# Groups of seven split b right behind a and use it second; landed tiles' splits stand in line in w_down's first units

## The chip, the cores and the metric

The kernel runs on one core of one Trainium2 chip. The metric is device microseconds of one execution of the whole program. The engines that count here are TensorE (PE), VectorE (DVE), ScalarE (ACT), GpSimd (POOL) and SyncE (SP, which issues most transfers). Each engine works through its own list of instructions in program order; semaphores make one engine wait for another. Weights come from DRAM by DMA. SBUF is the on-chip memory of 128 partitions, PSUM the memory in which matmuls accumulate, used in banks of 128 x 512 f32.

## The reference

One decoder layer for one sequence of 256 tokens, model width 2048, all f32:

```python
def reference(x, ...):
    mix = hybrid_mixer(rmsnorm(h, norm_mix_pre), w_in, ..., w_out)   # state-space heads beside attention heads
    h = h + rmsnorm(mix, norm_mix_post)
    ff = squared_relu_mlp(rmsnorm(h, norm_mlp_pre), w_up, w_down)
    h = h + rmsnorm(ff, norm_mlp_post)

def squared_relu_mlp(u, w_up, w_down):
    hdn = jax.nn.relu(jnp.einsum('bsd,df->bsf', u, w_up))            # 2048 -> 8192
    return jnp.einsum('bsf,fd->bsd', hdn * hdn, w_down)              # 8192 -> 2048
```

Most of the work is matmuls with large f32 weights that are each used for 256 tokens only (w_in, w_out, w_up, w_down).

## The kernel before

**Products in three parts.** A weight tile `raw` (two blocks of 128 rows by 512 columns, `[128, 2, 512]`) is split into `hi`, a rounded copy made by ACT (L150), and `lo = raw - hi`, made by DVE (L151). Activations lie as pairs too: `ah/al`, `sh/sl` or `ua`. A product is three matmuls of 128x512: hi with a_h, lo with a_h, hi with a_l. `parts` gives hi and lo from rings of 5 buffers each. Weights land in a ring of 4 `raw` buffers and in whatever other SBUF tiles are free at that time (`room["raw"]`: `mw`, `ha`, `uc` and so on), taken by turn in `fetch_next`; a buffer's next transfer waits until its last reader is done.

**Units.** The function `unit` computes two neighbouring blocks of 512 output columns for both tiles of 128 tokens. It goes over steps of 256 input rows in a written order. A step is either direct (`row_tiles`, L382 to L384: two weight tiles and 24 matmuls) or a group of seven (`seven`): the 2x2x2 blocks of weight and activation are combined so that seven products of 21 matmuls (L469 to L471) do the work of eight. The up units have 7 planned steps of which four are groups of seven, and one last direct step; the first units of w_down have 14 planned steps with six groups of seven and two last direct steps.

**A group of seven** needs these operands of the two weight tiles raw_a and raw_b. The first half of raw_b does not come from the weight as it is: POOL adds two blocks of rows in a DRAM tile called `pair`, and raw_b fetches that sum, so it can be used as it lands.

- a: raw_a, two halves; b: raw_b, two halves (the DRAM sum and a plain block)
- e: two differences that DVE makes (L275): e[1] = raw_a[0] + raw_b[0], then e[0] = e[1] - raw_b[1]
- t: t4 = e[1] + raw_a[1] (L275, `r<-e,raw` in the trace)

Each is split by `split_in_line`. `in_line` chains these instructions: each is issued on ACT and DVE behind the one chained before it, whatever the scheduler would prefer. Four products start sums of their own in `more[0..3]` and run through all groups of seven of a unit; the other three add into `acc`, where the direct steps add too. Behind the last group of seven, `combine_new` (L478 to L482) or `combine_onto` (L1152 to L1160) distributes `more[0..3]`: first a copy of more[0], then a subtraction of more[2], then more[3] and more[1].

**Activations of a group of seven** are combined as well (`sums_of_acts`, L428 to L431 on DVE, and a split), one step ahead.

**Hidden activations.** At the end of an up unit `up_end` puts a generator `turned` into `beside` for each block of 128 tokens by 512 columns: relu (L1522), square (L1523) and a 16-bit copy (L1515) on ACT, a transposing DMA from SP, and after its `yield`, a copy back (L1515) and the split into `ah/al` (L150 and L151), from which w_down's matmuls read. `pump_beside` runs the first half of one, `land_beside` the second, at the steps in TURNS and LANDS. In the first units of w_down the copies are placed exactly (`room["exact"]`): they are chained by `in_line`, between a group's splits and the next step's. The split behind the copy back is not: the scheduler places it among all that is ready. In half 1 the `halves` buffers of `turned` are parts of an SBUF tile `ha`, which later joins the ring of weight buffers (`more_in_place`), and a weight's transfer into it waits for the last al split that reads it.

The program runs the up units and two w_down units for one half of the 8192 hidden columns, then again for the other half. The six groups of seven of w_down's first unit start on PE between 953.8 (the first) and 1005.8 us (the last) in half 0, and between 1288.8 and 1347.9 in half 1.

Of the kernel before, what the change touches and what calls it, by code (L numbers as in the profile page):

```python
# [10 lines left out]
F32 = mybir.dt.float32  # L11
# [33 lines left out]
AHEAD = 1_000_000  # L45
# [35 lines left out]
def hymba_layer(ctx: ExitStack, tc: tile.TileContext, x, norm_mix_pre, w_in, conv_w, conv_b, dt_bias, a_log,  # L81
# [34 lines left out]
    def part(k):  # L116
        if k < NK:
            return sh, sl, k
        i, r = divmod(k - NK, NK // 2)
        return (*att[i], r)  # L120
# [14 lines left out]
    def bank():  # L135
        return pacc.tile([P, NB], F32, name="acc")

    def psmall():
        return psm.tile([P, NB], F32, name="ps")
# [7 lines left out]
    def split(hi, lo, src, scale=None):  # L147

        if scale is None:
            return (nc.scalar.activation(hi, src, AF.Copy),  # L150
                    nc.vector.tensor_tensor(lo, src, hi.bitcast(F32), op=ALU.subtract))  # L151
        return (nc.scalar.activation(hi, src, AF.Copy, scale=scale),
                nc.vector.scalar_tensor_tensor(lo, src, scale, hi.bitcast(F32), op0=ALU.mult, op1=ALU.subtract))
# [16 lines left out]
    def tmp():  # L170
        if "own" in room:
            room["own"].rotate(1)
            return room["own"][0]
        return hp.tile([P, NB], F32, name="r", bufs=4)

    def sum_tile():
        return room["sum"] if "own" in room else hp.tile([P, KB, NB], F32, name="e")
# [3 lines left out]
    room = {}  # L181
# [52 lines left out]
    def fetch_next(src, k0, c0, pair=None):  # L234

        turn = room["turn"]
        room["turn"] += 1
        n = turn % (RAWS + len(room["raw"])) - RAWS
        into = None if turn < 0 or n < 0 else room["raw"][n]
        with ExitStack() as order:  # L240
            for last in loaded if room.get("chain") else ():
                order.enter_context(tc.issue_after(last.ins))
            return fetch(src, k0, c0, into=into, pair=pair)

    def parts():
        return [wp.tile([P, KB, NB], F32R, name=n, bufs=BUFS) for n in ("hi", "lo")]
# [13 lines left out]
    @contextmanager  # L260
    def in_line():

        with ExitStack() as order:
            for last in line.values():
                order.enter_context(tc.issue_after(last.ins))
            yield

    def split_in_line(hi, lo, raw):
        with in_line():
            line["act"], line["dve"] = split(hi, lo, raw)  # L270
            newest["act"] = line["act"]

    def add_in_line(dst, a, b, op=ALU.add):
        with in_line():
            line["dve"] = nc.vector.tensor_tensor(dst, a, b, op=op)  # L275
# [33 lines left out]
    def pair_of(src, ca, k):  # L309

        next_pair()
        s_, c_, k_, d = paired[turn_of["pair"]]
        assert (s_ is src) and (c_, k_) == (ca, k), (c_, k_, ca, k)
        turn_of["pair"] += 1
        return d
# [103 lines left out]
    def sums_of_acts(k):  # L419

        if k in sums_of:
            return sums_of[k]
        places = room["sums"][2 * len(sums_of):][:2]
        h_, l_, r = room["acts"](k * KB)
        with tc.high_priority(offset=AHEAD):
            a, c = (tmp().rearrange("p (i s) -> p i s", s=P) for _ in range(2))
            ah_, al_ = (v[:, r:r + KB].bitcast(F32).rearrange("p j (t s) -> p j t s", t=NT) for v in (h_, l_))
            nc.vector.tensor_tensor(a.rearrange("p (j t) s -> p j t s", t=NT), ah_, al_, op=ALU.add)  # L428
            nc.vector.tensor_tensor(c[:, 0:2], a[:, 0::3], a[:, 1:2].to_broadcast([P, 2, P]), op=ALU.subtract)
            nc.vector.tensor_tensor(c[:, 2], a[:, 0], c[:, 1], op=ALU.add)  # L430
            nc.vector.tensor_tensor(c[:, 3], a[:, 2], c[:, 2], op=ALU.subtract)  # L431
            ch, cl = (v.rearrange("p b (t s) -> p (b t) s", t=NT) for v in places)
            split(ch, cl, c)
        sums_of[k] = ch, cl
        return ch, cl

    def seven(src, ca, cb, k, acc, more, first, last):


        ch, cl = sums_of_acts(k)  # L440
        h_, l_, r = room["acts"](k * KB)
        with tc.high_priority(offset=AHEAD):
            raw_a = fetch_next(src, k * KB, ca)
            raw_b = fetch_next(src, k * KB, cb, pair_of(src, ca, k))
            e, t4 = sum_tile(), tmp()
            add_in_line(e[:, 1], raw_a[:, 0], raw_b[:, 0])
            add_in_line(e[:, 0], e[:, 1], raw_b[:, 1], ALU.subtract)
            hl_a = parts()
            split_in_line(*hl_a, raw_a)
            add_in_line(t4, e[:, 1], raw_a[:, 1])  # L450
            hl_e = parts()
            split_in_line(*hl_e, e)
            hl_b = parts()
            split_in_line(*hl_b, raw_b)
            hl_t = parts()
            split_in_line(*(v[:, 0] for v in hl_t), t4)

        def block(j, t):
            return tuple(v[:, r + j, t * P:(t + 1) * P] for v in (h_, l_))

        def summed(i):
            return ch[:, i], cl[:, i]

        for dst, (a_h, a_l), (hi, lo), j, own in (
                (more[0], block(0, 0), hl_a, 0, True), (acc[0], block(1, 0), hl_a, 1, False),
                (more[1], summed(1), hl_e, 0, True), (more[2], summed(2), hl_e, 1, True),
                (more[3], summed(0), hl_b, 0, True), (acc[1], summed(3), hl_b, 1, False),
                (acc[2], block(1, 1), hl_t, 0, False)):
            nc.tensor.matmul(dst, a_h, hi[:, j], start=own and first, stop=False)  # L469
            nc.tensor.matmul(dst, a_h, lo[:, j], start=False, stop=False)  # L470
            nc.tensor.matmul(dst, a_l, hi[:, j], start=False, stop=own and last)  # L471
# [74 lines left out]
    def gemm_features(src, c0, begun=None, pumps=(1,)):  # L546


        acc = features()
        for k0 in range(0, NK, KB):  # L550
            hi, lo = weights(src, k0, c0) if k0 or begun is None else begun

            edges = k0 in (0, NK - KB)
            for fs in [(f,) for f in range(4)] if edges else [range(4)]:
                products(acc, hi, lo, k0, [(f, j) for f in fs for j in range(KB)])
            pump(pumps[k0 // KB % len(pumps)])
        return acc
# [397 lines left out]
    def attention(ap, h, qT, kT, v):  # L955
# [30 lines left out]
        for j, p in enumerate(turned):  # L986
            pair[j] = ap.tile([P, 3 * P], F32, name="pT", bufs=4)
            nc.scalar.activation(pair[j], p[:, :3 * P], AF.Copy)
# [343 lines left out]
    acc = [bank() for _ in range(2 * NT)]  # L1332
# [44 lines left out]
    more = [psmall(), bank(), psmall(), bank()]  # L1377
# [12 lines left out]
    acc, more = more, acc  # L1390
# [109 lines left out]
    def up_end(fb, b):  # L1500

        def at_end(t, acc):
            with tc.high_priority(offset=AHEAD):
                r = room["shared"][b][t]
                nc.vector.tensor_tensor(r, acc, r, op=ALU.subtract if b else ALU.add)
            beside.append(turned(t, 4 * fb, r))
        return at_end

    def perhaps_in_line(dst, src):

        if not room["exact"]:
            nc.scalar.activation(dst, src, AF.Copy)
            return
        with tc.high_priority(offset=AHEAD), in_line():
            newest["act"] = line["act"] = nc.scalar.activation(dst, src, AF.Copy)  # L1515

    def turned(t, k, r):
        room["halves"].rotate(1)
        halves = room["halves"][0]
        ts = slice(t * P, (t + 1) * P)  # L1520
        words = r.bitcast(U16)
        nc.scalar.activation(r, r, AF.Relu, scale=rmlp[:, t:t + 1])  # L1522
        nc.scalar.activation(r, r, AF.Square)  # L1523
        perhaps_in_line(halves.rearrange("p (h n) -> p h n", h=2), words.rearrange("p (n h) -> p h n", h=2))
        nc.sync.dma_start_transpose(words.rearrange("p (n s) -> p n s", s=P), halves)
        yield
        perhaps_in_line(halves.rearrange("p (n h) -> p h n", h=2), words.rearrange("p (h n) -> p h n", h=2))
        d_h, d_l, i = part(k)
        split(d_h[:, i:i + 4, ts], d_l[:, i:i + 4, ts], halves.bitcast(F32).rearrange("p (f s) -> p f s", f=4))

    def onto_new_mw(more):

# [6 lines left out]
    acc = gemm_features(w_up, NB, begun)  # L1539
# [6 lines left out]
    acc, more = [bank() for _ in range(2 * NT)], [psmall(), bank(), psmall(), bank()]  # L1546
    for hf in range(2):
        if hf:
            beside_up([], 0)
        for fb in range(0 if hf else 2, 8, 2):  # L1550
# [4 lines left out]
            acc, more = more, acc  # L1555
# [75 lines left out]
```

## Time and profile before

| | |
|---|---|
| median of 3 runs | 1460.96 us (1460.77 to 1460.99) |
| the profiled execution's own time | 1460.29 us |
| its span on the core | 1458.5 us |
| mean granted TensorE clock | 0.996 |
| DMA | 340.30 MB, mean 233 GB/s |
| groups of seven | 87, of 21 matmuls each |

The profile is one execution, taken by the hardware profiler. The page lists busy time of each engine, the span in 40 slices, the chain of work that ended last and the costliest groups of instructions. A row of the timeline reads: start in us, length in us, engine, line, operation, output<-inputs, shape, count; in brackets the idle time of the engine ahead of it and what ended it. Matmul ends are modelled, so a matmul's length is read from the distance between two starts. A window row reads: from and to in us, length, busy us and instructions of PE, its weight loads, DVE, ACT and POOL, the granted clock, the share of the DMA engines and GB/s.

### The profile page before, as it was taken

To read this page: it belongs to the slowest core of one execution; us is meant where nothing else is said; L and a number is where in the kernel's file an instruction comes from. 1 tells how busy PE (TensorE), PEld (TensorE's weight loads), DVE (VectorE), ACT (ScalarE), POOL (GpSimd) and SP (SyncE) were. 2 spreads that over 40 slices of the span, in tenths; PEclk is the share of its full clock that TensorE was granted. 3 is DMA by queue.
4 is the path that set the end of the run, shared out by engine and by line. 5 is a ranking of instruction groups with operands and counts; after the bars stand their busy time and mean duration, and the time that the engine had idled before them with its cause. 6 is when DMAs were issued, how large, how long until landed. Compare 5 with 4: busy or idle time off the path is not lost.

```text
span 1458.5 us, 20230 instructions
## 1 busy us (share of the span) xinstructions
PE 1437.7 (99%) x6930; PEld 1207.1 (83%) x6930; DVE 1297.9 (89%) x1881; ACT 1001.3 (69%) x1407; POOL 162.3 (11%) x244
## 2 busy tenths in 40 slices
PE   9999999999999999999999999999999999998998
PEld 8888888888888888888888888887888888876786
DVE  6798888988999788689989999999889999987998
ACT  6577669666666666566657679976565799876564
POOL 0201110131111000011100111010111111001000
PEclk9999999999999999999999999999999999999999
DMA  7977656756888647588976799698788999998855
GB/s 256 276 218 225 186 173 185 238 173 195 235 249 244 196 131 237 183 270 262 267 232 211 222 342 291 186 256 273 203 252 263 266 268 278 254 259 250 275 181 173
DMA packets 201926, 340.30 MB, mean 233 GB/s; under 512 B 45616, under 2 KB 48544, under 8 KB 201824
## 3 DMA queue, kind: packets, MB, share of 16 engines
q1 hardware_dynamic: 174304, 279.72, 61.4%
q0 software_dynamic: 19648, 45.63, 15.5%
q10 hardware_dynamic: 7872, 13.68, 2.8%
q8 instruction: 54, 0.88, 0.2%
q14 instruction: 48, 0.39, 0.1%
HBM read 327.39 MB, written 49.84 MB: 259 GB/s over the span
## 4 chain that ended last, share of the span: by engine, by line
PE 65%; DVE 6%; ACT 3%; issue 2%; DMA 2%; SPq 0%; DVEq 0%; ACTq 0%
PE acc L384 9%; PE acc L382 9%; PE acc L383 9%; PE acc L469 6%; PE acc L470 6%; PE acc L471 6%; PE acc L540 4%; DVE lo L151 3%; PE ps L384 2%; PE ps L382 2%; PE ps L383 2%; PE acc L543 2%; PE ps L471 2%; PE ps L470 2%; PE ps L469 2%
## 5 line engine op out<-in xcount | busy, mean ns | idle before, releaser
L151 DVE TENSOR_TENSOR lo<-raw,hi 128x1024 fp32r<-128x1024 f32 (+1 forms) x392 | 475.4, 1217 | 84.6 <-ACT hi L150 82.5
L150 ACT ACTIVATE hi<-raw 128x1024 fp32r<-128x1024 f32 (+1 forms) x392 | 408.0, 1048 | 181.6 <-PE acc L384 58.1
L540 PE MATMUL acc<-ua,hi 128*128 128x512 f32 x520 | 142.1, 402 | 0.0
L150 ACT ACTIVATE hi<-e 128x1024 fp32r<-128x1024 f32 x66 | 70.0, 1061 | 61.0 <-DVE e L275 55.5
L540 PEld LDWEIGHTS acc<-ua,hi 128*128 128x128 f32 x520 | 91.8, 190 | 14.1
L382 PE MATMUL acc<-hi,ua 128*128 128x512 f32 x228 | 90.0, 395 | 0.0
L383 PE MATMUL acc<-lo,ua 128*128 128x512 f32 x228 | 89.2, 391 | 0.0
L384 PE MATMUL acc<-hi,ua 128*128 128x512 f32 x228 | 89.1, 391 | 0.0
L382 PE MATMUL acc<-hi,sh 128*128 128x512 f32 x220 | 86.4, 393 | 0.0
L384 PE MATMUL acc<-hi,sl 128*128 128x512 f32 x220 | 85.7, 389 | 0.0
L383 PE MATMUL acc<-lo,sh 128*128 128x512 f32 x220 | 85.6, 389 | 0.0
L543 PEld LDWEIGHTS acc<-ua,lo 128*128 128x128 f32 x520 | 77.0, 190 | 9.0
L151 DVE TENSOR_TENSOR lo<-e,hi 128x1024 fp32r<-128x1024 f32 x66 | 80.4, 1217 | 0.9 <-ACT hi L150 0.7
L543 PE MATMUL acc<-ua,lo 128*128 128x256 f32 x520 | 79.2, 282 | 0.0
L469 PE MATMUL acc<-hi,ah 128*128 128x512 f32 x180 | 70.1, 390 | 4.1 <-ACT hi L150 4.1
L470 PE MATMUL acc<-lo,ah 128*128 128x512 f32 x180 | 70.4, 391 | 0.0
L471 PE MATMUL acc<-hi,al 128*128 128x512 f32 x180 | 70.3, 390 | 0.0
L540 PE MATMUL acc<-uc,hi 128*128 128x512 f32 x208 | 61.4, 405 | 0.0
L150 ACT ACTIVATE hi<-ha 128x1024 fp32r<-128x1024 f32 x46 | 48.2, 1051 | 15.8 <-DMA ha<-in_w_down_dram 6.2
L151 DVE TENSOR_TENSOR lo<-ha,hi 128x1024 fp32r<-128x1024 f32 x46 | 55.7, 1218 | 2.7 <-ACT hi L150 2.6
L150 ACT ACTIVATE hi<-r 128x512 fp32r<-128x512 f32 x66 | 41.2, 625 | 18.3 <-PE acc L384 8.5
L469 PE MATMUL acc<-hi,ua 128*128 128x512 f32 x137 | 53.5, 390 | 0.0
(578 smaller groups left out, 3739.0 us busy)
## 6 DMA issues: line engine op xcount, KB each, us to landing
raw<-in_w_in_dram SPq DMA_DIRECT2D x154, 512.0 KB, 4.6
raw<-in_w_down_dram SPq DMA_DIRECT2D x70, 512.0 KB, 5.4
raw<-in_w_up_dram SPq DMA_DIRECT2D x65, 512.0 KB, 5.1
raw<-in_w_out_dram SPq DMA_DIRECT2D x38, 512.0 KB, 5.1
raw<-pair SPq DMA_DIRECT2D x61, 256.0 KB, 4.3
pair<-in_w_up_dram POOLq DMA_DIRECT2D x56, 256.0 KB, 6.1
pair<-in_w_down_dram POOLq DMA_DIRECT2D x52, 256.0 KB, 5.8
ha<-in_w_up_dram SPq DMA_DIRECT2D x25, 512.0 KB, 5.7
```

What stands on the lines that cost most here:

```text
L150: return (nc.scalar.activation(hi, src, AF.Copy), nc.vector.tensor_tensor(lo, src, hi.bitcast(F32), op=ALU.subtract))
L151: nc.vector.tensor_tensor(lo, src, hi.bitcast(F32), op=ALU.subtract))
L382: nc.tensor.matmul(dst[:, cs], a_h[:, r, ts], hi[:, j, cs], start=begin and j == 0, stop=False)
L383: nc.tensor.matmul(dst[:, cs], a_h[:, r, ts], lo[:, j, cs], start=False, stop=False)
L384: product[t] = nc.tensor.matmul(dst[:, cs], a_l[:, r, ts], hi[:, j, cs], start=False, stop=end and j == KB - 1)
L469: nc.tensor.matmul(dst, a_h, hi[:, j], start=own and first, stop=False)
L470: nc.tensor.matmul(dst, a_h, lo[:, j], start=False, stop=False)
L471: nc.tensor.matmul(dst, a_l, hi[:, j], start=False, stop=own and last)
L540: nc.tensor.matmul(acc[f], hi[:, j, f * P:(f + 1) * P], u(k0 + j), start=k0 + j == 0, stop=False, skip_group_check=True)
L543: nc.tensor.matmul(acc[f][:, 0], lo[:, j, f * P:(f + 1) * P], u(k0 + j)[:, 0], start=False, stop=k0 + j == NK - 1, skip_group_check=True)
```

## The change

In `seven` the split of raw_b moves from behind the split of e to directly behind the split of raw_a, ahead of t4's addition. On PE the two products with b become the third and fourth, the two with e the fifth and sixth. In `turned`, where placement is exact, the split behind the copy back becomes a `split_in_line` at high priority: ah directly behind the copy on ACT, al directly behind the DVE instruction chained last. No operand, product or transfer is added or removed.

```diff
@@ seven
             hl_a = parts()
             split_in_line(*hl_a, raw_a)
+            hl_b = parts()
+            split_in_line(*hl_b, raw_b)
             add_in_line(t4, e[:, 1], raw_a[:, 1])
             hl_e = parts()
             split_in_line(*hl_e, e)
-            hl_b = parts()
-            split_in_line(*hl_b, raw_b)
             hl_t = parts()
             split_in_line(*(v[:, 0] for v in hl_t), t4)
...
                 (more[0], block(0, 0), hl_a, 0, True), (acc[0], block(1, 0), hl_a, 1, False),
+                (more[3], summed(0), hl_b, 0, True), (acc[1], summed(3), hl_b, 1, False),
                 (more[1], summed(1), hl_e, 0, True), (more[2], summed(2), hl_e, 1, True),
-                (more[3], summed(0), hl_b, 0, True), (acc[1], summed(3), hl_b, 1, False),
                 (acc[2], block(1, 1), hl_t, 0, False)):
@@ turned
-        split(d_h[:, i:i + 4, ts], d_l[:, i:i + 4, ts], halves.bitcast(F32).rearrange("p (f s) -> p f s", f=4))
+        whole = halves.bitcast(F32).rearrange("p (f s) -> p f s", f=4)
+        if not room["exact"]:
+            split(d_h[:, i:i + 4, ts], d_l[:, i:i + 4, ts], whole)
+            return
+        with tc.high_priority(offset=AHEAD):
+            split_in_line(d_h[:, i:i + 4, ts], d_l[:, i:i + 4, ts], whole)
```

How this moves instructions is seen in the order in which each engine gets them. First ACT in the first w_down unit of half 0, from the splits of one group of seven to the next step's split; `hi<-e` and `hi<-r` are the splits of e and t4, the `hi<-raw` next to `hi<-e` that of raw_b, and the two L1515 rows the copy back of one landing tile and the copy of the next tile to be turned. Before:

```order
L150 ACTIVATE hi<-raw 128x1024
L150 ACTIVATE hi<-e 128x1024
L150 ACTIVATE hi<-raw 128x1024
L150 ACTIVATE hi<-r 128x512
L1515 ACTIVATE mw_6209<-hb 128x2x512
L1522 ACTIVATE wpost<-wpost,rmlp 128x512
L150 ACTIVATE ah_3798<-mw_6209 128x4x128
L1523 ACTIVATE wpost<-wpost 128x512
L1515 ACTIVATE mw_6209<-wpost 128x1024
L150 ACTIVATE hi<-raw 128x1024
```

And now:

```order
L150 ACTIVATE hi<-raw 128x1024 x2
L150 ACTIVATE hi<-e 128x1024
L150 ACTIVATE hi<-r 128x512
L1515 ACTIVATE mw_6209<-hb 128x2x512
L150 ACTIVATE ah_3798<-mw_6209 128x4x128
L1522 ACTIVATE wpost<-wpost,rmlp 128x512
L1523 ACTIVATE wpost<-wpost 128x512
L1515 ACTIVATE mw_6209<-wpost 128x1024
L150 ACTIVATE hi<-raw 128x1024
```

The split of raw_b moved ahead of that of e, and ah moved ahead of the relu of the next tile.

Second, DVE in the last group of seven of that unit and behind it; `al` is the low part of landed tiles, L479 the first subtraction of `combine_new`. Before:

```order
L275 TENSOR_TENSOR r<-e,raw 128x512
L151 TENSOR_TENSOR lo<-e,hi 128x1024
L151 TENSOR_TENSOR lo<-raw,hi 128x1024
L151 TENSOR_TENSOR lo<-r,hi 128x512
L151 TENSOR_TENSOR lo<-raw,hi 128x1024
L151 TENSOR_TENSOR lo<-mw_6211,hi 128x1024
L151 TENSOR_TENSOR lo<-raw,hi 128x1024 x3
L151 TENSOR_TENSOR al_3799<-mw_6209,ah_3798 128x4x128 x2
L479 TENSOR_TENSOR r<-mw_6209,acc 128x512
```

Now there is no al there; the last one stands in the group before, directly behind L428. From there to the end of the same place:

```order
L151 TENSOR_TENSOR lo<-r,hi 128x512
L428 TENSOR_TENSOR r<-ah_3798,al_3799 128x512
L151 TENSOR_TENSOR al_3799<-mw_6209,ah_3798 128x4x128
L429 TENSOR_TENSOR r<-r 128x256
L151 TENSOR_TENSOR lo<-mw_6211,hi 128x1024
L430 TENSOR_TENSOR r<-r 128x128
L151 TENSOR_TENSOR lo<-raw,hi 128x1024
L431 TENSOR_TENSOR r<-r 128x128
L275 TENSOR_TENSOR e<-raw 128x512
L275 TENSOR_TENSOR e<-e,raw 128x512
L151 TENSOR_TENSOR wpost<-r,wpost 128x512
L151 TENSOR_TENSOR lo<-raw,hi 128x1024 x2
```

The last two al moved one and two groups forward, each into the line behind its ah, and the `lo` of raw_b (the second of the x2) moved from behind `lo<-e` to ahead of t4's addition.

## The prediction on record

> **What bounds the kernel now.** First I read the busy shares of the page, then the windows (a table of busy time by stretch), then the rows of the timeline at each hole.
>
> ```profile
> PE 1437.7 (99%) x6930; PEld 1207.1 (83%) x6930; DVE 1297.9 (89%) x1881; ACT 1001.3 (69%) x1407; POOL 162.3 (11%) x244
> ```
>
> TensorE (PE) is busy for 1437.7 of 1458.5 us, so the change, which neither adds nor removes a matmul, can only move the 20.8 us of holes and the stretches at a low clock. The windows say where those are; the columns are the busy time of each engine with its count, the granted clock, the DMA share and rate.
>
> ```profile
> 940.00:960.00 20.00, 20.00 (x90) 16.58 (x89) 19.37 (x28) 13.84 (x17) 1.91 (x3) 1.00 0.95 255
> 980.00:1000.00 20.00, 19.72 (x87) 16.34 (x88) 19.96 (x28) 16.01 (x19) 2.73 (x4) 1.00 0.86 240
> 1000.00:1020.00 20.00, 16.56 (x68) 13.21 (x67) 16.94 (x23) 10.62 (x12) 1.36 (x2) 0.93 0.97 301
> 1300.00:1320.00 20.00, 18.05 (x76) 13.79 (x75) 18.30 (x27) 17.12 (x21) 1.90 (x3) 1.00 1.08 278
> 1340.00:1360.00 20.00, 14.34 (x51) 10.83 (x50) 11.33 (x15) 9.75 (x11) 1.35 (x2) 0.83 0.94 290
> ```
>
> A full stretch holds 90 matmuls in 20 us. The last rows give the three holes that the change can reach, all in the first unit of w_down in each half: 1000 to 1020 lacks 22 matmuls, 1300 to 1320 lacks 14, 1340 to 1360 lacks 39. At 20.00 / 90 = 0.222 us each (0.227 between starts in the timeline) they are 5.0, 3.2 and 8.8 us. The first row of the timeline at each hole names the waited-for thing in brackets.
>
> ```profile
> 1015.98 0.50 PE L384 MATMUL ps<-hi,al 128*128 128x512 f32 x1 [3.44 <-DVE al L151]
> 1017.30 0.63 PE L382 MATMUL ps<-hi,ah 128*128 128x512 f32 x1
> 1017.73 0.63 PE L383 MATMUL ps<-lo,ah 128*128 128x512 f32 x1
> 1014.10 1.22 DVE L151 TENSOR_TENSOR lo<-raw,hi 128x1024 fp32r<-128x1024 f32 x1 [1.60 <-ACT hi L150]
> 1015.24 1.28 DVE L151 TENSOR_TENSOR al<-mw,ah 128x512 fp32r<-128x512 f32 x2
> 1013.01 1.06 ACT L150 ACTIVATE hi<-raw 128x1024 fp32r<-128x1024 f32 x1 [1.87 <-DMA raw<-in_w_down_dram]
> 999.76 0.61 ACT L150 ACTIVATE ah<-mw 128x512 fp32r<-128x512 f32 x1
> ```
>
> **Hole 1 (half 0).** PE waits 3.44 us for al, the low part of hidden activations. Its input ah was there at 1000.4, but VectorE (DVE) does both last al in one run only at 1015.24, behind a lo that waits for ACT's hi, which waits 1.87 us for a weight from DRAM. Behind the wait the matmuls start 0.43 us apart instead of 0.227.
>
> ```profile
> 1347.89 0.50 PE L469 MATMUL acc<-hi,ah 128*128 128x512 f32 x1 [4.11 <-ACT hi L150]
> 1350.36 0.80 PE L469 MATMUL acc<-hi,ub 128*128 128x512 f32 x1 [1.55 <-ACT hi L150]
> 1357.02 0.39 PE L471 MATMUL ps<-hi,al 128*128 128x512 f32 x1
> 1336.62 0.61 ACT L150 ACTIVATE ah<-ha 128x512 fp32r<-128x512 f32 x1
> 1339.86 0.68 DVE L151 TENSOR_TENSOR al<-ha,ah 128x512 fp32r<-128x512 f32 x1
> 1337.49 3.44 SPq L164 DMA_DIRECT2D ha<-in_w_down_dram  x3
> 1346.78 1.06 ACT L150 ACTIVATE hi<-ha 128x1024 fp32r<-128x1024 f32 x1 [6.17 <-DMA ha<-in_w_down_dram]
> 1349.08 1.22 DVE L151 TENSOR_TENSOR lo<-ha,hi 128x1024 fp32r<-128x1024 f32 x1
> ```
>
> **Hole 2 (half 1).** The last group of seven of the unit takes its first weight into the buffer ha, in which landed activations lie until their al (the last one's ah ends at 1337.2, its al only at 1340.5, 3.3 us later). So that buffer's DMA is issued late, ACT waits 6.17 us for it, and PE 4.11 and 1.55 us.
>
> **The change part by part.** All counts stay: no matmul, split or DMA is added or removed.
>
> *1. The order inside a group of seven.* One loop of half 0, on ACT and then on DVE:
>
> ```profile
> 959.67 1.06 ACT L150 ACTIVATE hi<-e 128x1024 fp32r<-128x1024 f32 x1 [1.87 <-DVE e L275]
> 961.59 0.61 ACT L150 ACTIVATE hi<-r 128x512 fp32r<-128x512 f32 x1
> 962.10 1.37 ACT L1515 ACTIVATE mw<-hb 128x1024 uint16<-128x1024 uint16 x1
> 963.33 0.70 ACT L1522 ACTIVATE wpost<-wpost,rmlp 128x512 f32<-128x512 f32 x1
> 964.45 0.62 ACT L1523 ACTIVATE wpost<-wpost 128x512 f32<-128x512 f32 x1
> 965.10 1.06 ACT L1515 ACTIVATE mw<-wpost 128x1024 uint16<-128x1024 uint16 x1
> 958.89 0.69 DVE L275 TENSOR_TENSOR e<-e,raw 128x512 f32<-128x512 f32 x1
> 959.50 1.22 DVE L151 TENSOR_TENSOR lo<-raw,hi 128x1024 fp32r<-128x1024 f32 x1
> 960.63 0.69 DVE L275 TENSOR_TENSOR r<-e,raw 128x512 f32<-128x512 f32 x1
> 967.14 1.22 DVE L151 TENSOR_TENSOR lo<-raw,hi 128x1024 fp32r<-128x1024 f32 x1 [0.76 <-ACT hi L150]
> 982.60 0.69 DVE L275 TENSOR_TENSOR e<-e,mw 128x512 f32<-128x512 f32 x1
> ```
>
> The loop comes back to the second e after (982.60 - 958.89) / 2 = 11.86 us, while a step of 45 matmuls takes PE 45 x 0.227 = 10.2: here ACT and DVE set the pace, and PE lives on its lead. The ring of that pace runs e (DVE), hi<-e, hi<-r, copy back, the rest of ACT's block, hi<-raw, lo<-raw (DVE idles 0.76 for it), next e. Now the split of b goes ahead of t4 (the r<-e,raw row). On ACT that is free: hi_b fits into the 1.87 us of idle ahead of hi<-e. On DVE a second lo stands ahead of t4, which moves from 960.63 to 959.50 + 2 x 1.13 = 961.76 (1.13 is the distance 960.63 - 959.50) and ends at 962.4. hi<-r, which starts at 961.59, can then start at about 962.53: **+0.94 us** on the ring. Everything queued on ACT behind hi<-r (copy back, relu, square, second copy, next hi) is as much later, and DVE's next lo waits for that. In loops without this block ACT has the room, and DVE's work is the same in sum: nothing.
>
> PE takes the b products as numbers 3 and 4, the e products as 5 and 6. Both positions need their lo after 6 and 12 matmuls as before, and lo_b, lo_e come in that order: no new wait. The second e product ends 6 matmuls (1.4 us) later; L479 needs it behind the last group of a unit. The copy L478 and one split on DVE ahead of L479 (1.22 in the rows above) take about 1 us of that; 0.4 us is left, and PE has a direct step's 24 matmuls on other banks to cover it. Without that cover it would be 0.4 a unit.
>
> *2. al in line.* ah now stands directly behind the copy back, so it waits for that copy to end (1.37 instead of the 1.23 us to the next start: +0.14), and relu and square stand back to back (0.65 instead of 0.60: +0.05). al waits on DVE until ah ends; what DVE does then (the r rows of L429 to L431, splits of weights) is queued behind it, for about 0.1 to 0.2 us. With part 1 a loop is 0.94 + 0.19 + 0.15 = **about 1.3 us** longer. A land-only loop (the fourth and fifth) pays the 0.6 us of al and hi_t's delay where it paid neither before: also about 1.3.
>
> *The sum of half 0.* Five loops make DVE up to 6.5 us later; the lead at each step comes off. The leads here are the start of the first matmul on a lo less that lo's end, first of the 969.01 below with the lo of 967.14 that ends at 968.36: 0.65 us.
>
> ```profile
> 969.01 0.39 PE L383 MATMUL ps<-lo,sh 128*128 128x512 f32 x1
> 980.28 0.50 PE L383 MATMUL ps<-lo,sh 128*128 128x512 f32 x1 [0.52 <-DVE lo L151]
> 988.42 1.22 DVE L151 TENSOR_TENSOR lo<-raw,hi 128x1024 fp32r<-128x1024 f32 x1
> 990.39 0.39 PE L383 MATMUL ps<-lo,ah 128*128 128x512 f32 x1
> 998.45 1.22 DVE L151 TENSOR_TENSOR lo<-mw,hi 128x1024 fp32r<-128x1024 f32 x1
> 1000.59 0.39 PE L383 MATMUL ps<-lo,ah 128*128 128x512 f32 x1
> ```
>
> The next has none (PE already waits at 980.28), then 990.39 less 989.64 is 0.75 and 1000.59 less 999.67 is 0.92. So PE is later by 1.3 - 0.65 = 0.65, then 2.6, 3.9 - 0.75 = 3.15, and 5.2 - 0.92 = about **4.2 us** before the hole. The hole goes, since al is done a loop earlier and PE, 4.2 us later, meets the weight that landed at 1013.0: **-5.0**. Half 0: **-0.8**.
>
> *The sum of half 1.* The same loops, with less lead (14 matmuls are lost in 1300 to 1320 already), make PE about 3.8 us later by the last group. The last al ends at about 1340.7 where it ended at 1340.5: in line it is 2.6 us earlier in its loop (behind ah it would end 0.7 us after it, not 3.3), and the loops are as much later, about 2 x 1.3 above their leads. So the DMA into ha is issued and lands when it did, PE resumes at about 1350.3, and what PE lost on the way is taken off the wait of 4.11 us: no gain. What is left are waits of 0.3 and 1.9 us with matmuls between. Does the clock fall behind it? Rows on both sides: behind the 3.44 us it fell; in 1300 to 1320, with several waits under 1 us, it stays 1.00. Mine is nearer to the latter, so I take no fall. From 1350.36 to the end of the group's last start (1357.02 + 0.23) 20 matmuls took 6.9 us; at full pace they take 4.5, and lo_e of that group comes about 0.2 us too late for that (two lo of 1.13, t4 and lo_e behind 1349.08): **-2.2**; with a fall 0.
>
> The Trainium skill has a rule for this place: "TensorE: Matmul & The Clock Gate", section "What's actually happening", lets the clock fall to half after an idle window of some 3.4 us and rise again after as long a busy one, counted in a free-running window. The 3.44 us row with its 0.43 us starts agrees; by it the remaining waits cost no clock (sum -3.0), and only if PE arrived more than 3 us earlier than I have it would they (sum -0.8).
>
> *Elsewhere.* In the up units and the second w_down units DVE's sum is the same and hi_t has ACT's idle time behind it: 0, bounded by -0.8 (the wait at 980.28, should it go) and +6 (rival 3).
>
> **Sum:** -0.8 - 2.2 = -3.0 against the profiled execution's own 1460.29 (span 1458.5 and 1.79 around it), 1457.3. The median is 0.67 above that execution, so 1460.96 - 3.0 = **1458.0 us**.
>
> **Rivals.** A measurement tells about 0.2% (2.9 us) from no change; faster is below 1458.0, slower above 1463.9.
>
> *Rival 1: the loops don't get longer.* Then hole 1 goes for nothing (-5.0), al in line is 2.6 us earlier in half 1, and so is the DMA into ha (-2.6), with the clock -2.2: 1460.96 - 9.8 = 1451.2; with half the lengthening about 1455. For it: ACT idles 1.87 us in each loop and is busy only 16.01 of 20 us at 980 to 1000. Against: that idle time lies ahead of hi<-e, the delay comes after it.
>
> *Rival 2: the clock falls anyway, or ha comes a us or two later* than I chained it, since each loop carries its delay into the last al: it costs 2.2 to 4 us of the forecast: 1460.2 to 1462.0.
>
> *Rival 3, slower: t4 behind a second split costs in the up units too.* There are 28 groups of seven in the up units (four in each of seven), each with hi_t 0.94 us later on ACT.
>
> ```profile
> DVE lo L151 <- ACT hi L150: 101.1, 127, 2.5
> ACT hi L150 <- DVE e L275: 55.5, 35, 2.5
> ```
>
> These rows of the waits (us in all, times, longest) say that DVE waits for ACT's hi 127 times already, and ACT for e 35 times. If ACT's following hi is late for DVE by only a third of the 0.94 in these 28, PE, whose leads there are 0.3 to 1 us in tight places, loses up to 28 x 0.31 = 8.7 us, less leads of some 3: +3 to +6 where the forecast has 0, and with it rival 2's: 1464 to 1468. It decides once ACT's idle time behind hi_t is under 0.9 us. Against it: where hi_b stood between hi<-e and hi<-r it now is gone from there, which gives ACT the time back. Beside this, the same skill page, section "Architectural detail: the array is 16× 32×32, not 1× 128×128", calls ACT and DVE strict FIFO; that speaks against putting al in line, since an al that waits holds all of DVE behind it. The lo of 1014.10 ahead of al shows just that; with al in line the price in my sum is 0.15 us a loop, by this rule it is as much as ah is late.
>
> **How the numbers follow.** Forecast 0.40, with its own range of 1456 to 1460, half of it (0.20) below 1458.0. Rival 1 0.23, all faster. Rival 2 0.17, all within. Rival 3 0.20, of which 0.19 slower and 0.01 within. Faster 0.43, same 0.38, slower 0.19. The range leaves out the far end of rival 1 (under 1452.5, 0.08) and of rival 3 (above 1465.5, 0.10).
>
> **What would show it.** Right: in the timeline near 1015 no wait of PE for al, and al rows one by one, each behind the r row of L428; hi<-r about 3.6 us behind the start of the second e instead of 2.7; the loop at about 13.1 us; more short waits of PE for lo from 965 to 1010; near 1350 waits of 2 to 3 us in place of 5.7 and a clock over 0.9. Wrong: loops at 11.9 us (rival 1), the window at 1340 to 1360 at 0.83 again (rival 2), windows of up units below 90 matmuls (rival 3).

## The result, and the profile after

The changed kernel takes 1477.89 us (median of 4 runs, 1473.9 to 1484.64) beside 1460.97 for the kernel before (4 runs): a ratio of 1.0118, 95% interval 1.0079 to 1.0158. It is slower by 17 us, where 3 us faster was forecast, and its runs now lie 11 us apart; those of before lay 1.7 apart. The profiled execution took 1476.38 us.

The page's first row and the windows of the changed kernel, the columns as before:

```profile
PE 1443.2 (98%) x6930; PEld 1203.8 (82%) x6930; DVE 1301.5 (88%) x1881; ACT 1002.0 (68%) x1407; POOL 162.5 (11%) x244
```

```profile
880.00:900.00 20.00, 16.57 (x65) 13.01 (x64) 13.55 (x18) 13.96 (x18) 2.71 (x4) 0.91 0.98 230
900.00:920.00 20.00, 18.12 (x80) 14.44 (x79) 16.95 (x22) 13.29 (x17) 1.89 (x3) 1.00 0.94 246
1000.00:1020.00 20.00, 19.62 (x84) 15.23 (x83) 19.19 (x28) 14.22 (x17) 2.12 (x4) 1.00 0.84 230
1220.00:1240.00 20.00, 16.35 (x72) 12.98 (x70) 14.26 (x16) 15.37 (x20) 1.90 (x3) 1.00 0.99 239
1240.00:1260.00 20.00, 18.92 (x74) 14.94 (x75) 17.48 (x22) 14.91 (x19) 2.16 (x3) 0.91 0.81 206
1320.00:1340.00 20.00, 17.00 (x65) 12.60 (x64) 16.19 (x23) 16.74 (x20) 2.17 (x3) 0.91 1.03 270
```

The stretches from 880 to 920 and from 1220 to 1260 are up units; both were full before. Against 90 matmuls for each 20 us, the changed kernel lacks 35 of them between 860 and 960 and 39 between 1180 and 1280, where 0 and 2 were missing. That is 72 more, at 0.222 us 16 us: the whole loss. In w_down's first unit of half 0 (960 to 1060) 32 are missing where 29 were, in that of half 1 (1280 to 1400) 53 where 56 were. There the change does nothing on balance.

What happens in the up units is read at the first hole. ACT, SP, DVE and PE of the changed kernel in the timeline (L1512 is the 16-bit copy of `turned` where it is not chained, as in the up units; L1525 is the transposing DMA):

```profile
884.64 0.62 ACT L150 ACTIVATE hi<-r 128x512 fp32r<-128x512 f32 x1
890.72 1.34 ACT L1512 ACTIVATE mw<-wpost 128x1024 uint16<-128x1024 uint16 x1 [5.47 <-DMA wpost<-mw]
892.63 1.04 ACT L150 ACTIVATE hi<-raw 128x1024 fp32r<-128x1024 f32 x1
876.71 0.63 SPq L159 DMA_DIRECT2D ha<-pair  x1
877.39 0.42 SPq L160 DMA_DIRECT2D ha<-in_w_up_dram  x1
879.22 1.51 SPq L164 DMA_DIRECT2D ha<-in_w_up_dram  x2
880.79 3.58 SPq L1525 DMA_TRANSPOSE wpost<-mw  x1
892.76 0.69 DVE L151 TENSOR_TENSOR sl<-mw,sh 128x512 fp32r<-128x512 f32 x1 [5.89 <-ACT sh L150]
893.73 0.50 PE L382 MATMUL ps<-hi,uc 128*128 128x512 f32 x1 [2.67 <-ACT hi L150]
894.99 0.50 PE L383 MATMUL ps<-lo,uc 128*128 128x512 f32 x1 [0.76 <-DVE lo L151]
```

The same tile in the kernel before:

```profile
885.66 0.62 ACT L150 ACTIVATE hi<-r 128x512 fp32r<-128x512 f32 x1
886.18 1.37 ACT L1512 ACTIVATE mw<-wpost 128x1024 uint16<-128x1024 uint16 x1
875.86 1.23 SPq L1525 DMA_TRANSPOSE wpost<-mw  x1
```

Read them from the transpose on. Before, SP issued it at 875.9, and the copy back of that tile, at 886.2 on ACT, did not wait. Now it stands on SP behind the three rows of transfers into ha and goes out at 880.8. On ACT the copy back follows hi<-r at once, and waits 5.47 us for the transpose. Everything behind it on ACT waits too, the split sh and the next hi<-raw among it, so DVE idles 5.89 us and PE 2.67 and 0.76, with a clock of 0.91 in this window.

The next tile's first copy and copy back (`junk`), in the changed kernel and then before, show the other thing that moved:

```profile
895.00 1.04 ACT L1512 ACTIVATE mw<-junk 128x1024 uint16<-128x1024 uint16 x1
904.70 1.37 ACT L1512 ACTIVATE mw<-junk 128x1024 uint16<-128x1024 uint16 x1 [4.24 <-DMA junk<-mw]
```

```profile
882.80 1.06 ACT L1512 ACTIVATE mw<-junk 128x1024 uint16<-128x1024 uint16 x1
893.33 1.36 ACT L1512 ACTIVATE mw<-junk 128x1024 uint16<-128x1024 uint16 x1
```

The copy back was the 12th instruction of ACT behind the first copy and did not wait. Now it is the 5th and waits 4.24 us. The view of a line gives the sum: whoever waited for the transposes of L1525. For the changed kernel

```profile
who waited for it (us, times):
  ACT ha L1512: 13.9, 4
  ACT mw L1512: 9.7, 2
...
DMA to landing us min/median/max: 2.7/6.4/10.4
```

and for the kernel before nobody. (The last row is the time from a transpose's issue to its landing.) A second wait is new there. The waits of both kernels from 840 to 950 us (us in all, times, longest) have in the changed kernel, and not before:

```profile
ACT hi L150 <- DVE r L275: 6.7, 5, 1.8
...
ACT mw L1512 <- DMA wpost<-mw: 5.5, 1, 5.5
ACT mw L1512 <- DMA junk<-mw: 4.2, 1, 4.2
```

The first row is hi<-r waiting for t4, the delay that the prediction had for w_down's loops.

### The profile page after: what moved, and what is told of

Read it like the earlier page. It is cut to its first block, busy times and chain, and to the rows that moved or that the text cites. A ratio compares the mean times of both kernels' runs of the same rounds, so it can differ in the third digit from the quotient of the medians.

```text
span 1474.6 us, 20217 instructions
## 1 busy us (share of the span) xinstructions
PE 1443.2 (98%) x6930; PEld 1203.8 (82%) x6930; DVE 1301.5 (88%) x1881; ACT 1002.0 (68%) x1407; POOL 162.5 (11%) x244
## 4 chain that ended last, share of the span: by engine, by line
PE 52%; DVE 11%; ACT 6%; DMA 5%; issue 3%; SPq 0%; ACTq 0%; DVEq 0%
PE acc L382 7%; PE acc L384 7%; PE acc L383 7%; DVE lo L151 6%; PE acc L470 4%; PE acc L469 4%; PE acc L471 4%; PE acc L540 4%; ACT hi L150 3%; PE acc L543 2%; DVE e L275 2%; DMA raw<-in_w_down_dram 2%; PE ps L470 2%; PE ps L469 2%; PE ps L471 2%
## 5 line engine op out<-in xcount | busy, mean ns | idle before, releaser
L382 PE MATMUL acc<-hi,ua 128*128 128x512 f32 x228 | 90.1, 395 | 0.0
L384 PE MATMUL acc<-hi,ua 128*128 128x512 f32 x228 | 89.2, 391 | 0.0
L383 PE MATMUL acc<-lo,ua 128*128 128x512 f32 x228 | 89.1, 391 | 0.0
L470 PE MATMUL acc<-lo,ua 128*128 128x512 f32 x137 | 53.4, 390 | 0.5 <-DVE lo L151 0.5
```

What stands on the lines that cost most here:

```text
L382: nc.tensor.matmul(dst[:, cs], a_h[:, r, ts], hi[:, j, cs], start=begin and j == 0, stop=False)
L383: nc.tensor.matmul(dst[:, cs], a_h[:, r, ts], lo[:, j, cs], start=False, stop=False)
L384: product[t] = nc.tensor.matmul(dst[:, cs], a_l[:, r, ts], hi[:, j, cs], start=False, stop=end and j == KB - 1)
```

## The experiments

"Lacks" below counts missing matmuls against 90 per 20 us in the windows of the profiled run. Experiments were run in groups; those of a group share a chip and the runs of the kernel before on it, and each ratio is to these. Lines are named as in the kernel before. The theories that the expectations name: A, the loss is made in the up units, where copies back wait for transposes; B, al in line makes it; C, hi<-r's longer wait for t4 makes it; D, the new order of the splits starves PE wherever the transposes stand.

**The order of splits and products alone.** The changed kernel with `turned` as before:

```diff
-        with tc.high_priority(offset=AHEAD):
-            split_in_line(d_h[:, i:i + 4, ts], d_l[:, i:i + 4, ts], whole)
+        split(d_h[:, i:i + 4, ts], d_l[:, i:i + 4, ts], whole)
```

> Only the order of the splits and products in a group of seven (first part of the change); al is split as before, wherever the scheduler puts it. Theory A (the loss is made in the up units: with the new order the transposes stand further back among SP's transfers and the copies back stand directly behind hi<-r on ACT, which then waits for them): the up units lose what they lose in the changed kernel, 72 matmuls or 16 us, and w_down's first units lose hole 1 (5 us) or not as al falls: 1474 to 1482 us. Theory B (al in line holds DVE and costs the time): 1458 to 1464 us.

Measured: 1478.34 us beside 1458.75, ratio 1.0134 (1.0102 to 1.0166). L1512 waits 21.1 us for transposes, the up units lack 78. The loss belongs to the first part of the change.

**al in line alone.** The kernel before with the new `turned`:

> Only al in line (second part of the change), splits and products of a group as before. Theory A: the up units run as before, hole 1 is gone (-5.0), a loop costs about 0.3 more for ah and al (+1 to +2), and in half 1 the DMA into ha goes out up to 2.6 us earlier: 1454 to 1458 us. Theory B: 1470 us or more.

Measured: 1449.80 us, ratio 0.9935 (0.9914 to 0.9956): the second part by itself is a gain of 9 us, more than either theory had. In its windows hole 1 is gone, and hole 2, which falls between 1320 and 1340 here, lacks 10 matmuls where it lacked 39:

```profile
1000.00:1020.00 20.00, 20.00 (x90) 16.53 (x89) 18.86 (x24) 10.86 (x12) 1.35 (x2) 1.00 0.77 236
1320.00:1340.00 20.00, 18.28 (x80) 14.67 (x79) 17.93 (x27) 12.28 (x14) 1.36 (x2) 1.00 0.64 194
```

The last al of half 1 starts at 1329.5 instead of 1339.9, the transfer into ha goes out with it, and PE waits 1.72 us at the last group of seven where it waited 4.11 and 1.55:

```profile
1329.52 0.68 DVE L151 TENSOR_TENSOR al<-ha,ah 128x512 fp32r<-128x512 f32 x1
1330.23 0.37 SPq L164 DMA_DIRECT2D ha<-in_w_down_dram  x1
1339.23 0.50 PE L469 MATMUL acc<-hi,ub 128*128 128x512 f32 x1 [1.72 <-ACT hi L150]
```

**Both parts, the new order only in w_down.** In `seven` the order now depends on the unit:

```diff
+        late_e = src is w_downs[0] or src is w_downs[1]
...
+            if late_e:
+                hl_b = parts()
+                split_in_line(*hl_b, raw_b)
             add_in_line(t4, e[:, 1], raw_a[:, 1])
             hl_e = parts()
             split_in_line(*hl_e, e)
-            hl_b = parts()
-            split_in_line(*hl_b, raw_b)
+            if not late_e:
+                hl_b = parts()
+                split_in_line(*hl_b, raw_b)
```

(and the products alike).

> Both parts, but the new order of splits and products only in the units of w_down; everywhere else the old order. Theory A: the up units keep their 90 matmuls in 20 us, and w_down's units run as in the changed kernel, where half 0 lacks 32 matmuls instead of 29 and half 1 53 instead of 56: 1459 to 1462 us. Theory C (t4 behind the second split is slow by itself, wherever it stands, and the up units are hit no worse than others): 1466 us or more.

Measured: 1457.32 us, ratio 0.9989 (0.9978 to 1.0001). That is a little below theory A's range, and far from theory C's. The up units lack 4. So the new order costs about 19 us outside w_down (0.9989 of before against 1.0118), some 16 of them in the up units (4 missing matmuls against 74; another new wait of the changed kernel, 1.06 us for L481, stands at 274 us), and about 7.5 us in w_down (1457.32 less 1449.80), where it eats most of what al in line gains.

**t4 ahead of the split of b.** The changed kernel with

```diff
             split_in_line(*hl_a, raw_a)
+            add_in_line(t4, e[:, 1], raw_a[:, 1])
             hl_b = parts()
             split_in_line(*hl_b, raw_b)
-            add_in_line(t4, e[:, 1], raw_a[:, 1])
```

> The changed kernel, but t4 is added ahead of the split of b instead of behind it (a, t4, b, e, t); products with b still second. Theory C (hi<-r waits for t4, 0.94 us longer in each group): that wait is gone, loops of w_down take 11.9 to 12.2 us again, time 1452 to 1458 us. Theory A says only that it depends on where transposes and copies back come to stand; they stand earlier on SP here than in the changed kernel, so the up units lose less than half of the 72 matmuls: 1455 to 1466 us. If moving b itself costs: 1474 us or more.

Measured: 1453.22 us, ratio 0.9963 (0.9951 to 0.9975). Loops take 12.1 to 12.2 us, hi<-r's wait for t4 falls to 2.0 us from 840 to 950 and L1512's wait for transposes to 2.7 in all; the up units lack 5. One DVE instruction in another place takes back about 23 us (0.9963 of before against 1.0118). The time lies in theory C's range and 2 us below theory A's. Both waits fall here, so the run does not say which of them costs what.

**The transposes at high priority.** The changed kernel with

```diff
-        nc.sync.dma_start_transpose(words.rearrange("p (n s) -> p n s", s=P), halves)
+        with tc.high_priority(offset=AHEAD):
+            nc.sync.dma_start_transpose(words.rearrange("p (n s) -> p n s", s=P), halves)
```

> The changed kernel, with one difference: the transposing DMAs are given the same high priority as the weights' transfers, so that the one that stood behind three transfers into ha on SP (issued at 880.8 us in the changed kernel, 875.9 before) stands ahead of them again; ACT's and DVE's orders stay. Theory A (SP issues the transposes late, and the copies back wait for them on ACT): the 23.6 us that L1512 waits for L1525 in the changed kernel fall below 8 us, the up units lack under 35 matmuls instead of 72, time 1462 to 1469 us. Theory D (the transposes' place doesn't matter, the order of the splits starves PE by itself): 1473 us or more.

Measured: 1465.30 us beside 1459.71, ratio 1.0037 (1.0026 to 1.0048); the up units lack 33. The wait for transposes fell to 13.3 us, not below 8. The hole at 893 is gone, a later one is left, since that tile's first copy still stands late on ACT:

```profile
880.00:900.00 20.00, 20.00 (x90) 16.52 (x88) 15.93 (x20) 13.90 (x18) 2.85 (x5) 1.00 1.05 278
900.00:920.00 20.00, 17.49 (x77) 13.99 (x76) 19.35 (x22) 18.25 (x24) 2.58 (x4) 1.00 0.99 260
```

SP's order, with the splits in the order of the changed kernel, is worth about 12 us (1.0037 of before against 1.0118). Theory D is out: the place of the transposes matters.

**The order of the products alone.**

```diff
-                (more[1], summed(1), hl_e, 0, True), (more[2], summed(2), hl_e, 1, True),
                 (more[3], summed(0), hl_b, 0, True), (acc[1], summed(3), hl_b, 1, False),
+                (more[1], summed(1), hl_e, 0, True), (more[2], summed(2), hl_e, 1, True),
```

> Al in line and the new order of the products on PE, with the splits in the old order (a, t4, e, b, t). Theory A: hi<-r comes 2.7 us after the second e again, the loops of w_down take 12.2 us, no copy back waits for a transpose: within 4 us of al in line alone, so 1449 to 1455 us; PE may wait for lo of b, which is made after that of e but used ahead of it, some 0.5 us a group where leads are short. If the order of the products carries the loss: 1465 us or more.

The expectation speaks of al in line, but the kernel that ran has al as before the change, so it stands against the kernel before. Measured: 1463.88 us, ratio 1.0030 (1.0018 to 1.0041). Holes 1 and 2 are there as before (4.05 and 4.57 us of wait), copies back wait 1.1 us for transposes in all, and PE waits for lo in up units (0.30 us at 904, 0.28 at 1200, 0.17 at 1215). With the old splits b's lo comes last, so using b second costs some 4 us.

**The order of the splits alone**, with products and `turned` as before:

> Only the splits of a group in the new order (a, b, t4, e, t), products in the old order and al as before. Theory A: the transposes stand on SP as in the changed kernel, L1512 waits over 15 us for them, time 1472 to 1484 us, like both orders together. If the new products order is needed for the loss: below 1465 us.

Measured: 1481.18 us, ratio 1.0149 (1.0125 to 1.0173); L1512 waits 19.2 us, the up units lack 83. The splits carry the loss.

**t4 ahead of all splits in w_down**, then a, b, e, t, with al in line; old order elsewhere:

> Al in line; in w_down's units t4 is added ahead of all splits, then a, b, e, t, products a, b, e, t; all other units as before. If hi<-r's wait for t4 is what sets the loops' length: hi<-r comes 1.75 us after the second e (2.70 before, 3.68 in the changed kernel), the loops take 11.2 to 11.4 us (12.2 with al in line alone), and most of the 5 us that PE still lacks there go: 1445 to 1449 us. If DVE is the limit instead: loops stay at 12 us, 1449 to 1453 us.

Measured: 1449.41 us beside 1459.71, ratio 0.9938 (0.9920 to 0.9957). hi<-r comes 1.75 us behind the second e as expected, and two of the loops fall to 11.5 us, near it, but the time is that of al in line alone and above the range that went with shorter loops. From 960 to 1060 it lacks 12 matmuls (al in line alone: 9), 5 of them from 1020 to 1040, where PE waits 0.90 us for L1477 (the addition into mw at the end of a unit), and from 1280 to 1360 it lacks 29 (28).

**The last group of each unit in the old order**, otherwise as the run before:

> Al in line, t4 ahead of all splits in w_down's units as in the run before of that kind, but the last group of seven of each unit in the old order, so that the bank that L479 and L1477 read is finished 6 matmuls earlier. If that wait (0.9 us at 1028 us) is what took back the gain of the shorter loops: 1446 to 1449 us; if not: 1449 to 1452 us.

Measured: 1451.04 us beside 1460.96, ratio 0.9939 (0.9921 to 0.9957): the same. The wait for L1477 is gone, and other holes are larger (1300 to 1320 has 69 matmuls). Where the shorter loops' gain goes was not settled.

**The copies pinned in the up units too.** The changed kernel with

```diff
-                pump_beside(len(order) > 7)
+                pump_beside(True)
...
-                land_beside(len(order) > 7 and i > 0)
+                land_beside(i > 0)
```

> The changed kernel with the order of splits and products kept everywhere, but with the copies and splits of the hidden activations pinned in line in the up units too, as they are in w_down's first units. That puts at least 14 of ACT's instructions between a tile's first copy and its copy back in every up unit (as few as 5 in the changed kernel, 12 or more before except at the end of half 1), and the transposes ahead on SP. Theory A (copies back that come too soon behind the transposes): L1512 and L1515 wait under 4 us for transposes in all, the up units lack under 20 matmuls instead of 72, time near that of the new order in w_down alone: 1456 to 1462 us. Theory D (the new order starves PE in the up units by itself): 1470 us or more.

Measured: 1504.47 us, ratio 1.0307 (1.0292 to 1.0323), a clear miss. Nobody waits for a transpose any more, yet PE loses more. From 840 to 960 us the waits of this kernel say why:

```profile
ACT hi L150 <- DVE r L275: 14.6, 9, 1.8
DVE lo L151 <- ACT hi L150: 14.5, 10, 2.6
...
ACT hb L1522 <- DVE hb L1505: 3.8, 2, 3.6
```

Pinned behind hi<-r, the copies make a loop of the up units as they do in w_down, with hi<-r's wait for t4 on it, and a relu that waits 3.6 us holds ACT. By its number the run lies in theory D's range, but it changed more than the copies' distance. No run pins the copies in the up units with the old order, so what the pinning costs by itself is not shown, nor how much of the loss is the wait for t4.

**The first half of a turned tile at high priority** (relu, square, first copy and transpose; nothing pinned), in the changed kernel:

```diff
+        with tc.high_priority(offset=AHEAD):
-        nc.scalar.activation(r, r, AF.Relu, scale=rmlp[:, t:t + 1])
+            nc.scalar.activation(r, r, AF.Relu, scale=rmlp[:, t:t + 1])
...
```

> The changed kernel, all orders of splits and products kept, with the first half of each turned tile (relu, square, first copy, transpose) at high priority and nothing pinned. ACT then has at least 9 instructions between a tile's first copy and its copy back in the up units (as few as 5 in the changed kernel), but for one at the end of half 1 with 4, as before. Theory A (copies back stand too close behind late transposes): L1512 waits under 8 us for transposes (23.6 in the changed kernel), the up units lack under 35 matmuls instead of 72: 1458 to 1467 us. Theory C (hi<-r's wait for t4 costs in the up units, with or without that): 1472 us or more.

Measured: 1466.68 us beside 1460.88, ratio 1.0050 (1.0032 to 1.0067). That is at the upper end of theory A's range. The wait for transposes is 9.3 us in all (under 8 was expected) and 2.7 from 840 to 950; the up units lack 25. hi<-r's wait is as long as ever:

```profile
ACT hi L150 <- DVE r L275: 8.8, 6, 1.8
...
ACT mw L1512 <- DMA junk<-mw: 2.7, 1, 2.7
```

**The same on al in line alone**, where it brings copies back closer:

> Al in line, splits and products in the old order, and the same high priority for the first half of each turned tile. Here it brings the copies back closer: 6 and 7 of ACT's instructions behind the first copy at three places of each group of up units, where al in line alone has 12 or more. Theory A: L1512 waits for transposes for 8 us or more though no split moved, and the time is 1455 us or more. If the order of the splits is needed for the loss: 1449 to 1452 us, as al in line alone.

Measured: 1452.25 us, ratio 0.9946 (0.9926 to 0.9966). L1512 waits 11.4 us for transposes, as expected, and in the profiled run, the slowest of five (1455.73 us), the up units lack 35 matmuls though no split moved and hi<-r does not wait for t4 there. The median is within the interval of al in line alone, against theory A's 1455 or more. The other runs have no profile, so what transposes cost in them is not known.

Side by side, from 840 to 950 us of the profiled runs (waits in us, missing matmuls against 487):

| kernel | L1512 for transposes | hi<-r for t4 | lacks |
|---|---|---|---|
| before; al in line alone | 0 | 0 | 0 |
| t4 ahead of b's split | 0.4 | 2.0 | 0 |
| changed, first halves at high priority | 2.7 | 8.8 | 8 |
| changed, transposes at high priority | 6.0 | 5.9 | 13 |
| al in line, first halves at high priority | 7.0 | 0 | 19 |
| changed | 9.7 | 6.7 | 35 |

In half 0 the missing matmuls go with the waits for transposes; the wait for t4, at 8.8 us beside 2.7, leaves 8. The row next to last is from that kernel's slowest run, so its 19 are probably more than such waits cost there as a rule. Half 1 adds what half 0 does not show, from 1180 to 1280 us:

| kernel | L1512 for transposes | hi<-r for t4 | lacks |
|---|---|---|---|
| before | 0 | 0 | 2 |
| t4 ahead of b's split | 2.3 | 2.6 | 4 |
| changed, first halves at high priority | 0 | 6.5 | 17 |
| changed, transposes at high priority | 7.3 | 1.0 | 20 |
| al in line, first halves at high priority | 4.3 | 0 | 17 |
| changed | 12.5 | 2.4 | 39 |

Here 17 matmuls are missing with no wait for a transpose, and 17 with none for t4. Each wait can cost without the other, as far as two single profiles of kernels in which the first halves moved too can show it.

## Why the prediction was wrong, point by point

- **The loops in w_down: right, to the size.** hi<-r was to come 3.6 us behind the second e and the loop to take 13.1 us. In the changed kernel:

```profile
967.78 0.69 DVE L275 TENSOR_TENSOR e<-e,raw 128x512 f32<-128x512 f32 x1
971.47 0.63 ACT L150 ACTIVATE hi<-r 128x512 fp32r<-128x512 f32 x1 [1.83 <-DVE r L275]
980.97 0.69 DVE L275 TENSOR_TENSOR e<-e,raw 128x512 f32<-128x512 f32 x1
```

  That is 3.69 and 13.19 us. The parts fit too: 12.86 us with the new order alone (+1.00, worked out 0.94), 12.20 with al in line alone (+0.34, worked out 0.19 and 0.15).
- **Hole 1: right.** No PE wait for al is left near 1015, and each al stands behind its L428. al waits 0.37 us for ah, where 0.1 to 0.2 was taken.
- **Hole 2: right in size, in part by luck.** At the last group of half 1 PE waits 2.04 and 0.29 us (1367 and 1368 us), where 0.3 and 1.9 were worked out in place of 4.11 and 1.55. But the long one is for another transfer: hi of the weight in ha waits 0.75 us on ACT and holds PE no more, and PE waits for hi of the tile in raw, whose own transfer is late:

```profile
1362.71 1.06 ACT L150 ACTIVATE hi<-ha 128x1024 fp32r<-128x1024 f32 x1 [0.75 <-DMA ha<-in_w_down_dram]
1366.15 1.06 ACT L150 ACTIVATE hi<-raw 128x1024 fp32r<-128x1024 f32 x1 [2.38 <-DMA raw<-in_w_down_dram]
1367.26 0.50 PE L469 MATMUL acc<-hi,ub 128*128 128x512 f32 x1 [2.04 <-ACT hi L150]
```

  Rival 1 (loops no longer) is out with the loops.
- **The sums of w_down: within the noise.** -0.8 and -2.2 were forecast, -3.0 in all. The new order in w_down alone with al in line gives -1.4 us (interval -3.2 to +0.1). The sum held two effects of opposite sign: al in line alone, at 0.9935 of 1460.96 or 1451.5 us, is where rival 1 (1451.2) put loops that do not get longer. "PE has a direct step's 24 matmuls on other banks to cover it" failed: PE waits 0.81 us for L1477 at 1042 in the changed kernel. And "I take no fall" held at the last group of half 1, but the clock fell ahead of it, behind the waits at 1323 us.
- **"Elsewhere ... 0, bounded by -0.8 and +6": the step that failed.** It says that in loops without the in-line block "ACT has the room". It had not: hi<-r waits for t4 in the up units too, and 17 matmuls are missing from 1180 to 1280 us in a kernel where that wait (6.5 us) stands without one for a transpose. And it left out the copies and transposes of the up units, which are pinned nowhere: with the new chain copies back stand as few as 5 ACT instructions behind the first copy of their tile (12 or more before, but for the end of half 1), and a transpose behind three rows of transfers on SP; L1512 waits 23.6 us for transposes where it waited for none. The up units lost 16 us where 0 was forecast. The order in which the engines get their instructions can be read before any run, on ACT and on SP; the prediction read it only in w_down.
- **Rival 3 had the place, the sign and a part of the cause.** It named the up units, hi<-r's delay and 3 to 6 us, with a chance of 0.20. The delay is there (6.7 us of waits from 840 to 950). With first halves at high priority 25 matmuls (5.6 us) are left of 74, 17 of them where no copy waits for a transpose; the rest of the loss, by copies back behind late transposes, the rival did not have. Its claim that each of 28 groups pays was wrong too: the loss stands in a few holes of each half.
- **How the 19 us divide** was bounded, not settled. With the transposes or the first halves at high priority 10 to 12 us of the loss go; 7 to 9 stay against the order in w_down alone, in kernels where both waits are left in part. Matmuls are missing beside each of the waits without the other (17 and 17 from 1180 to 1280 us). That they also make each other worse, ACT's slack being used up by the wait for t4 when a copy back holds ACT for 5 us, is likely but was not shown. Why the scheduler moved the copies was not tried.
- **The chances.** Faster had 0.43, slower 0.19. The two edits should have been summed apart: one alone gains 9 us, the other alone loses 20.

The rule of the Trainium skill that was weighed ("TensorE: Matmul & The Clock Gate", "What's actually happening") was not enough here. Behind waits of 1.66 and 0.53 us, with two matmuls between, the changed kernel's starts are 0.43 us apart for 3 us (granted clock 0.91 from 1320 to 1340):

```profile
1323.29 0.73 PE L382 MATMUL ps<-hi,sh 128*128 128x512 f32 x2 [1.66 <-ACT hi L150]
1324.55 0.50 PE L383 MATMUL ps<-lo,sh 128*128 128x512 f32 x1 [0.53 <-DVE lo L151]
...
1325.97 0.63 PE L383 MATMUL ps<-lo,sh 128*128 128x512 f32 x1
1326.40 0.63 PE L384 MATMUL ps<-hi,sl 128*128 128x512 f32 x1
...
1329.22 0.39 PE L382 MATMUL acc<-hi,sh 128*128 128x512 f32 x1
```

## What to carry to other kernels

A change in a chained order moves what is not chained: after such an edit compare the order on every engine, SP's transfers included, in all the units that run the code, and look for an instruction that waits for a DMA right behind the chain. Sum up the parts of a change one by one, and try them apart: here the part that looked like an aside was the gain, and no version was faster than al in line with the old order (0.9935 of before). Between an instruction that starts a DMA and the one that waits for it count what the engine has to do; with transposes that land 6.4 us (median) behind their issue, five instructions of about 1 us are not enough.

## What the runs showed of the hardware that was not expected

The clock fell without a single wait near 3.4 us: behind 2.67 and 0.76 us (894.99), and behind 1.66 and 0.53 us (1324.55), each time for 3.0 to 3.4 us of starts 0.43 us apart. The granted clock was 0.91 in both windows (880 to 900 and 1320 to 1340). Behind 2.04 and 0.29 us (1368.05) it did not fall: 1.00 from 1360 to 1380.
